# A decoder layer on one core: values spread by one copy each from ScalarE's queue, and two lags of the attention steps lengthened

## The chip, the cores and the metric

The kernel runs on one core of a Trainium2 chip. The metric is the device time of one execution in microseconds (us). TensorE (PE) multiplies, VectorE (DVE) and ScalarE (ACT) work on tiles of 128 partitions, GpSimd (POOL) does small vector work and issues accumulating transfers, and SyncE (SP) issues most transfers. ScalarE has a queue for transfers of its own.

## What is computed

One layer of a decoder trunk on 512 tokens of width 1024, all in float32. After a norm and one wide projection there are two mixers side by side, retention and a dilated attention in three groups of four heads; then an output projection, an MLP of width 4096 and a gated embedding term. The change touches the attention:

```python
for g, (window, dilation) in enumerate(((128, 1), (512, 4), (2048, 16))):
    # keys gathered by stride, own block and previous block, QK-norm and rotary before
    s = einsum(q_g, k_g) * hd ** -0.5          # masked to the window
    m = max(s); e = exp(s - m); l = sum(e)
    o_g = einsum(e / l, v_g); lse_g = m + log(l)
wts = softmax(stack(lse_g))                    # over the three groups
o = sum over g of wts_g * o_g                  # (512, 4 * 128)
```

All of it is in float32; where the kernel multiplies by weights, it does so in three products of operands split in a high and a low part.

## The kernel before, in words

**Products.** Each weight tile of 128x1024 floats (`raw`, 512 KB, loaded on SP at L212, for some with an addition by GpSimd's transfer at L228 or by DVE at L226) is split in two: ScalarE makes `whi` (L250), DVE then `wlo` = raw - whi (L251). Both have four buffers. A product is three matmuls (L262 to L264): whi, wlo, whi again with the other operand's low part. Many projections go by seven products of halves in place of eight (`seven_products`); a helper `after` takes each finished product out of its PSUM bank. Products have four PSUM banks (`pg`), and everything else (scores `sc`, transposes `pe`, `ph`, `pc`, weighted values `po`, and the products called `pa`) shares four others.

**Values.** `values_seven` makes the value rows for two groups at once. The part `m` of a product is finished by L757, L759 or L761, and for the products 6 and 7 the finished tile of 128 rows is spread by L764: every fourth row goes to another place in the 32 partitions of the strided value tile `v`, by four transfers of 32x512 floats (64 KB) each, on SP. It is called twice; each call has four such tiles, so that there are 32 transfers.

**Scores.** `scores(g, ...)` puts four blocks (`block(r)`) in a list of deferred steps. A block of groups 1 and 2 makes 128x512 scores in one bank (L787); group 0 has one such block and three of twice the width in two banks each (L795), seven banks in all. `softmax` masks them on DVE (L678, which frees the bank), takes the maximum (L681), scales it (L682, and L684 with the group before), and ScalarE makes exponentials `se` (L687, four of 128 columns or two of 256). `turn` transposes them (L694, four per block) when its lag is over; for group 2 it first forces `rescale`. `weigh_values` multiplies them with the values (L835).

**Rescaling.** `rescale(2, ...)` joins the groups' denominators: f (L863, its exponential on ScalarE at L864), w (L866), the sum (L867), the reciprocal `inv` (L870), f times inv (L871), and a copy `wide` (L878), all on DVE; ScalarE scales the last group's exponentials by inv, sixteen instructions at L876. TensorE transposes `wide` (`pc`, L884), ScalarE takes it out and writes it to DRAM (L886, L887), and reads it back spread over the partitions (L892); DVE multiplies the sum of the earlier groups by it (L897).

**What sets the order.** The program is written as one pass over the products. After each unit of product work `tick` advances a clock; deferred steps, put in by `later(lag, ...)` at the end of the list or by `prompt(lag, ...)` at its head, run when their lag is over, at most two for every two ticks. `force(key)` runs steps from the head of the list until the named one is done. A scheduler of the framework then arranges each engine's recorded instructions; that order is fixed when the kernel is built, and each engine runs its own list in order. ScalarE's rotation inputs `rz` (L987) and DVE's rotations (L575, L578, L580) are the retention keys' work, which lies beside.

Of the kernel before, what the change touches and what calls it, by code (L numbers as in the profile page):

```python
# [17 lines left out]
P = 128  # L18
S = 512
D = 1024  # L20
NT = S // P
# [6 lines left out]
DIL = 4  # L28
# [51 lines left out]
class Block:  # L80
# [618 lines left out]
    def attention(self):  # L699

        nc = self.nc
        with self.tc.manual_schedule(engines={nc.scalar.engine, nc.vector.engine}):
            qk = self.att_proj(0, 0), self.att_proj(0, 1)
        nc.sync.dma_start(self.mask, self.a["c_mask"])
        self.gain_rows(1, NG)
        self.rot_rows(1)
        self.spare = True
        self.left = self.token_factors_seven()
        rq = self.rq
        qk1 = self.att_proj(1, 0), self.att_proj(1, 1)  # L710
        pT = [self.big("pT") for _ in range(2)]
        first, turned = self.scores(0, *qk, rq, None, pT)
        strided = self.const.tile([P, NT, 2, H], F32, name="st0p")
        self.prompt(10, lambda: self.to_strided(first, strided))
        past, turned1 = self.scores(1, *qk1, self.rq, strided, None, 18)
        self.later(24, lambda: self.rescale(1, strided, past), ("past", 1))
        v0, v1 = self.values_seven((self.r, self.r_minus))
        for g, v, pTs, lag in ((0, v0, turned, 2), (1, v1, turned1, 8)):
            values = self.weigh_values(g, v, pTs)
            for r in range(NT):  # L720
                self.later(lag, lambda r=r, values=values: values(r), ("att", g, r))
        qk = self.att_proj(2, 0), self.att_proj(2, 1)
        last, turned = self.scores(2, *qk, self.rq, past, None, 14)
        self.later(21, lambda: self.rescale(2, past, last), ("past", 2))
        dec, kdec = self.decays()
        kd, v2 = self.values_seven((None, self.r_minus), self.ret_keys(kdec))
        values = self.weigh_values(2, v2, turned)
        for r in range(NT):
            self.later(5, lambda r=r, values=values: values(r), ("att", 2, r))
        return dec, kd  # L730

    def values_seven(self, scale, ready=None):

        nc = self.nc
        for j in range(2):
            self.force(("S", j))
        held, out = {}, {}

        def tile(n):
            if n not in out:  # L740
                out[n] = self.big("v")
            return out[n]

        def after(m, p, ps):
            t = p if m in (1, 2, 3, 6) else 2 + p
            main = m in (1, 2, 4)
            r = scale[0 if main else 1]
            by = {} if r is None else dict(scale=r[:, t : t + 1])
            if main:
                o = tile(0)[:, t]  # L750
            elif m in (3, 5):
                o = self.tmp("m3") if m == 3 else self.tabp.tile([P, 512], F32, tag="tab", name=self.nm("m5"))
                held[{3: 6, 5: 7}[m], p] = o
            else:
                o = held.pop((m, p))
            if m in (1, 3, 5, 4):
                nc.scalar.activation(o, ps, AF.Copy, **by)  # L757
            elif r is None:
                nc.vector.tensor_tensor(o, o, ps, op=ALU.add)  # L759
            else:  # L760
                nc.vector.scalar_tensor_tensor(o, ps, r[:, t : t + 1], o, op0=ALU.mult, op1=ALU.add)  # L761
            if m in (6, 7):
                for q in range(DIL):
                    nc.sync.dma_start(tile(1)[32 * t : 32 * (t + 1), q], o[q : P : DIL])  # L764
            if m in (2, 4) and ready is not None:
                ready(t, o)

        self.seven_products(self.left, after)
        return tile(0), tile(1)

    def scores(self, g, qT, kT, rq, past, held=None, lag=2):

        nc = self.nc
        st = self.const.tile([P, NT, 2, H], F32, name=f"st{g}")
        pTs = [[] for _ in range(NT)]
        self.es = {}
        slots = None if held is None else [b[:, i] for b in held for i in range(4)]

        def block(r):
            m, l = st[:, r, 0], st[:, r, 1]  # L780
            rs = slice(r * P, (r + 1) * P)
            es = []
            wide = g == 0 and r > 0
            if not wide:
                sc = self.bank("sc")
                for h in range(H):
                    nc.tensor.matmul(sc[:, h * P : (h + 1) * P], qT[:, h, rs], kT[:, h, rs], start=True, stop=True)  # L787
                es.append(self.softmax(sc, P, H, self.mask[:, 128 * (g + 1) : 128 * (g + 2)], rq[:, r], m, l,
                                       None if past is None else past[:, r, 0]))
                self.es[g, r] = es[0]  # L790
            else:
                for hp in range(2):
                    sc = self.bank("sc")
                    for h in range(2):
                        nc.tensor.matmul(sc[:, h * 256 : (h + 1) * 256], qT[:, 2 * hp + h, rs],  # L795
                                         kT[:, 2 * hp + h, (r - 1) * P : (r + 1) * P], start=True, stop=True)
                    hs = slice(2 * hp, 2 * hp + 2)
                    es.append(self.softmax(sc, 256, 2, self.mask[:, 0:256], rq[:, r, hs], m[:, hs], l[:, hs]))
            for e in es:
                self.later((5, 8, 11)[g], lambda e=e: turn(e, r), ("pT", g, r))  # L800

        def turn(e, r):
            if g == 2:
                self.force(("past", 2))
            if g == 1 and not self.pT1:
                self.pT1.append(self.big("pT"))
            out = slots.pop(0) if slots else self.pT1[0][:, r] if g == 1 else None
            pTs[r].append(self.transpose4(e, out))

        for r in range(NT):  # L810
            self.later(lag, lambda r=r: block(r), ("sc", g, r))
        return st, pTs
# [43 lines left out]
    def rescale(self, g, past, st):  # L856

        nc = self.nc
        for r in range(NT):
            self.force(("sc", g, r))  # L860
        t3 = lambda s: self.sm.tile([P, NT, H], F32, tag="sm16", name=self.nm(s))
        f, l = t3("f"), st[:, :, 1]
        nc.vector.tensor_tensor(f, st[:, :, 0], past[:, :, 0], op=ALU.subtract)  # L863
        nc.scalar.activation(f, f, AF.Exp)  # L864
        w = t3("w")
        nc.vector.tensor_tensor(w, f, past[:, :, 1], op=ALU.mult)  # L866
        nc.vector.tensor_tensor(l, l, w, op=ALU.add)  # L867
        if g == NG - 1:
            inv = t3("inv")
            nc.vector.reciprocal(inv, l)  # L870
            nc.vector.tensor_tensor(f, f, inv, op=ALU.mult)  # L871
            for r in range(NT):
                e = self.es[g, r]
                for h in range(H):
                    c = slice(h * P, (h + 1) * P)
                    nc.scalar.activation(e[:, c], e[:, c], AF.Copy, scale=inv[:, r, h : h + 1])  # L876
        wide = self.const.tile([P, H * NT], F32, name=f"wide{g}")
        nc.vector.tensor_copy(wide.rearrange("p (h r) -> p r h", h=H), f)  # L878
        d = self.dram.tile([H, S], F32, name=f"f_dram{g}", tag=f"f_dram{g}")
        spread = []  # L880

        def turn():
            ps = self.bank("pc")
            nc.tensor.transpose(ps[: H * NT, :P], wide, self.ident)  # L884
            turned = self.turned[: H * NT]
            nc.scalar.activation(turned, ps[: H * NT, :P], AF.Copy)  # L886
            nc.scalar.dma_start(d.rearrange("a (r l) -> (a r) l", r=DIL), turned)  # L887

        def load():
            spread.append(self.big("fb"))  # L890
            for h in range(H):
                nc.scalar.dma_start(spread[0][:, h], d[h : h + 1].to_broadcast([P, S]))  # L892

        def scale():
            for h in range(H):
                o = self.oT[0][:, h]
                nc.vector.tensor_tensor(o, o, spread[0][:, h], op=ALU.mult)  # L897

        self.later(1, turn)
        self.later(4, load)  # L900
        self.later(12, scale, ("scaled", g))


# [613 lines left out]
```

## Time and profile before

| | |
|---|---|
| median of 3 runs | 953.83 us (953.59 to 954.54) |
| profiled execution | 955.36 us |
| its span | 953.6 us |
| mean granted TensorE clock | 0.997 |

In the profile, L12 is line 12 of the kernel before. Busy shares are of the span; a row of the timeline has its start, its duration, the engine, the line, what it writes and from what, how many instructions it stands for, and in brackets how long the engine stood idle before it and what ended that. The part of the name behind the engine tells the queue: SPq and ACTq are transfers issued by SyncE and ScalarE, and their duration is that of issuing.

### The profile page before, as it was taken

How to read it: one execution, taken by the hardware profiler on the slowest of the kernel's cores; microseconds unless marked ns; L12 is line 12 of the kernel's file. 1: busy time of each engine (PE TensorE's matmuls, PEld its weight loads, DVE VectorE, ACT ScalarE, POOL GpSimd, SP SyncE). 2: the span in 40 equal slices, each digit the busy share in tenths (PEclk: the TensorE clock that was granted, in tenths of full speed). 3: DMA queues.
4: the chain of work that ended last, by engine and by line, in shares of the span. 5: the costliest groups of instructions: out<-in, count | busy, mean ns of one | idle time of the engine just before them, and what ended most of it. 6: DMA issues, size and time to landing. Idle time of an engine off the chain costs nothing.

```text
span 953.6 us, 14325 instructions
## 1 busy us (share of the span) xinstructions
PE 943.3 (99%) x5357; PEld 826.2 (87%) x5357; DVE 718.4 (75%) x997; ACT 562.1 (59%) x1065; POOL 159.5 (17%) x140
## 2 busy tenths in 40 slices
PE   9999999999899999999999999999999999999998
PEld 6888888888788888999988888988998998998887
DVE  7789964766697849386937889799499689769953
ACT  5657775445745566576714446884494486467651
POOL 0322210222001112223012211111212302112100
PEclk9999999999999999999999999999999999999999
DMA  9953466258437645869737677868958968876911
GB/s 333 282 170 82 106 141 215 64 118 195 148 111 155 173 100 138 163 181 217 232 115 236 148 178 214 206 153 222 199 156 202 191 183 157 224 172 159 288 50 56
DMA packets 92549, 162.87 MB, mean 171 GB/s; under 512 B 8608, under 2 KB 20544, under 8 KB 92480
## 3 DMA queue, kind: packets, MB, share of 16 engines
q1 hardware_dynamic: 65168, 113.37, 36.4%
q0 software_dynamic: 23936, 46.14, 29.0%
q10 hardware_dynamic: 3376, 2.44, 0.9%
q8 instruction: 42, 0.69, 0.3%
q14 instruction: 27, 0.22, 0.1%
HBM read 153.49 MB, written 6.34 MB: 168 GB/s over the span
## 4 chain that ended last, share of the span: by engine, by line
PE 92%; DVE 3%; ACT 1%; issue 1%; DMA 1%; POOL 1%; SPq 0%; ACTq 0%; POOLq 0%; DVEq 0%
PE pg L264 25%; PE pg L262 25%; PE pg L263 25%; PE pa L264 3%; PE pa L263 3%; PE pa L262 3%; PE po L835 1%; PE ph L590 1%; DVE wlo L251 1%; PE pe L694 1%; PE sc L787 1%; PE ry L1083 1%; PE kv L1070 1%; PE ry L1085 1%; DVE ro L578 0%
## 5 line engine op out<-in xcount | busy, mean ns | idle before, releaser
L251 DVE TENSOR_TENSOR wlo<-raw,whi 128x1024 fp32r<-128x1024 f32 (+1 forms) x258 | 306.8, 1198 | 112.7 <-ACT whi L250 111.8
L250 ACT ACTIVATE whi<-raw 128x1024 fp32r<-128x1024 f32 (+1 forms) x257 | 266.3, 1041 | 212.1 <-PE pg L264 87.2
L263 PE MATMUL pg<-f,whi 128*128 128x256 f32 x384 | 108.7, 283 | 0.0
L264 PE MATMUL pg<-f,wlo 128*128 128x256 f32 x384 | 108.7, 283 | 0.0
L262 PE MATMUL pg<-f,whi 128*128 128x256 f32 x384 | 108.7, 283 | 0.0
L262 PE MATMUL pg<-whi,hh 128*128 128x512 f32 x248 | 98.6, 398 | 0.0
L264 PE MATMUL pg<-whi,hl 128*128 128x512 f32 x248 | 97.1, 392 | 0.0
L263 PE MATMUL pg<-wlo,hh 128*128 128x512 f32 x248 | 96.8, 390 | 0.0
L262 PE MATMUL pg<-whi,f 128*128 128x512 f32 x192 | 75.4, 393 | 0.0
L263 PE MATMUL pg<-wlo,f 128*128 128x512 f32 x192 | 74.8, 389 | 0.0
L264 PE MATMUL pg<-whi,f 128*128 128x512 f32 x192 | 74.8, 389 | 0.0
L262 PEld LDWEIGHTS pg<-f,whi 128*128 128x128 f32 x384 | 73.7, 192 | 0.2
L263 PEld LDWEIGHTS pg<-f,whi 128*128 128x128 f32 x384 | 73.7, 192 | 0.2
L264 PEld LDWEIGHTS pg<-f,wlo 128*128 128x128 f32 x384 | 73.7, 192 | 0.0
L228 POOL DMA_DIRECT2D raw<-in_w_in x32 | 38.9, 1216 | 197.8 <-DVE wlo L251 193.0
L264 PEld LDWEIGHTS pg<-whi,hl 128*128 128x128 f32 x248 | 46.6, 188 | 9.8
L263 PEld LDWEIGHTS pg<-wlo,hh 128*128 128x128 f32 x248 | 46.6, 188 | 9.2
L262 PEld LDWEIGHTS pg<-whi,hh 128*128 128x128 f32 x248 | 46.6, 188 | 9.2
L228 POOL DMA_DIRECT2D raw<-in_w_down x24 | 29.0, 1215 | 139.3 <-DVE wlo L251 108.2
L262 PE MATMUL pg<-whi,us 128*128 128x512 f32 x128 | 52.1, 407 | 0.0
L228 POOL DMA_DIRECT2D raw<-in_w_up x24 | 29.0, 1211 | 135.0 <-DVE wlo L251 124.7
L264 PE MATMUL pg<-whi,us 128*128 128x512 f32 x128 | 50.0, 391 | 0.0
(280 smaller groups left out, 2298.0 us busy)
## 6 DMA issues: line engine op xcount, KB each, us to landing
raw<-in_w_in SPq DMA_DIRECT2D x72, 512.0 KB, 4.1
raw<-in_w_in POOLq DMA_DIRECT2D x32, 512.0 KB, 6.2
raw<-in_w_up SPq DMA_DIRECT2D x32, 512.0 KB, 4.6
raw<-in_w_down SPq DMA_DIRECT2D x32, 512.0 KB, 4.6
raw<-in_w_up POOLq DMA_DIRECT2D x24, 512.0 KB, 6.6
raw<-in_w_down POOLq DMA_DIRECT2D x24, 512.0 KB, 5.9
x<-in_x SPq DMA_DIRECT2D x8, 512.0 KB, 8.2
raw<-in_w_ret_out SPq DMA_DIRECT2D x8, 512.0 KB, 3.8
```

Source lines behind the costliest of these rows:

```text
L228: self.nc.gpsimd.dma_start(raw, self.chained[i].rearrange("(k p) n -> p k n", p=P), accum_op=ALU.add)
L250: self.pin(nc.scalar.activation(R(hi[:, i]), raw[:, i], AF.Copy))
L251: nc.vector.tensor_tensor(R(lo[:, i]), raw[:, i], hi[:, i], op=ALU.subtract)
L262: t.matmul(ps, sh, mh, start=first, stop=False, skip_group_check=more)
L263: t.matmul(ps, sh, ml, start=False, stop=False, skip_group_check=more)
L264: t.matmul(ps, sl, mh, start=False, stop=last, skip_group_check=more)
L590: self.nc.tensor.transpose(ps[:, t * P : (t + 1) * P], rots[t][:, h * HD : (h + 1) * HD], self.ident)
L694: self.nc.tensor.transpose(ps[:, k * P : (k + 1) * P], e[:, k * P : (k + 1) * P], self.ident)
L787: nc.tensor.matmul(sc[:, h * P : (h + 1) * P], qT[:, h, rs], kT[:, h, rs], start=True, stop=True)
L835: nc.tensor.matmul(po[:, h * P : (h + 1) * P], v[:, vt, h * HD : (h + 1) * HD], pt, start=b == 0, stop=b == len(blocks) - 1)
L1070: nc.tensor.matmul(ps, kd[:, n, hs], v[:, n, c], start=True, stop=True)
L1083: nc.tensor.matmul(y, sT[0][:, r], v[:, i, c], start=True, stop=i == 0)
```

## The change

There are four edits. Group 0's scores have a lag of 4 in place of 2. A finished value tile is spread by one transfer of 32x4x512 floats in place of four, as a prompt step with lag 2, from ScalarE's queue. The transposes of the last group's exponentials have a lag of 15 in place of 11. And `scale`, in `rescale`, first forces the weighing steps of the group before; as a new line it moves all later lines of the file by one (L898 was L897).

```diff
--- before.py
+++ after.py
@@ -709,7 +709,7 @@
         rq = self.rq
         qk1 = self.att_proj(1, 0), self.att_proj(1, 1)
         pT = [self.big("pT") for _ in range(2)]
-        first, turned = self.scores(0, *qk, rq, None, pT)
+        first, turned = self.scores(0, *qk, rq, None, pT, 4)
         strided = self.const.tile([P, NT, 2, H], F32, name="st0p")
         self.prompt(10, lambda: self.to_strided(first, strided))
         past, turned1 = self.scores(1, *qk1, self.rq, strided, None, 18)
@@ -760,8 +760,8 @@
             else:
                 nc.vector.scalar_tensor_tensor(o, ps, r[:, t : t + 1], o, op0=ALU.mult, op1=ALU.add)
             if m in (6, 7):
-                for q in range(DIL):
-                    nc.sync.dma_start(tile(1)[32 * t : 32 * (t + 1), q], o[q : P : DIL])
+                rows = tile(1)[32 * t : 32 * (t + 1)]
+                self.prompt(2, lambda: nc.scalar.dma_start(rows, o))
             if m in (2, 4) and ready is not None:
                 ready(t, o)
 
@@ -797,7 +797,7 @@
                     hs = slice(2 * hp, 2 * hp + 2)
                     es.append(self.softmax(sc, 256, 2, self.mask[:, 0:256], rq[:, r, hs], m[:, hs], l[:, hs]))
             for e in es:
-                self.later((5, 8, 11)[g], lambda e=e: turn(e, r), ("pT", g, r))
+                self.later((5, 8, 15)[g], lambda e=e: turn(e, r), ("pT", g, r))
 
         def turn(e, r):
             if g == 2:
@@ -892,6 +892,7 @@
                 nc.scalar.dma_start(spread[0][:, h], d[h : h + 1].to_broadcast([P, S]))
 
         def scale():
+            self.force(("att", g - 1, NT - 1))
             for h in range(H):
                 o = self.oT[0][:, h]
                 nc.vector.tensor_tensor(o, o, spread[0][:, h], op=ALU.mult)
```

Together with the scheduler this rearranges TensorE, DVE and ScalarE between some 101 and 330 us; SP only loses its 32 transfers, and GpSimd keeps its order. Numbers behind names only tell buffers apart, and differ between the two programs.

First ScalarE, at the last group's exponentials (`se` from L687), beside the splits of weights (`whi`). Before:

```order
L687 ACTIVATE se_2356,st_2159<-sm_2355,st_2159,rqs_1928 128x128 x4
L250 ACTIVATE whi_2459<-raw_2006 128x1024
L687 ACTIVATE se_2372,st_2159<-sm_2371,st_2159,rqs_1928 128x128 x4
L250 ACTIVATE whi_2463<-raw_2169 128x1024
L687 ACTIVATE se_2415,st_2159<-sm_2414,st_2159,rqs_1928 128x128 x4
L250 ACTIVATE whi_2557<-raw_2555 128x1024
L250 ACTIVATE whi_2563<-raw_2561 128x1024
L687 ACTIVATE se_2431,st_2159<-sm_2430,st_2159,rqs_1928 128x128 x4
L864 ACTIVATE f_2484<-f_2484 128x16
L987 ACTIVATE rz_2512<-v_2217,dec 128x128 x3
L876 ACTIVATE se_2356<-se_2356,inv_2490 128x128 x4
L876 ACTIVATE se_2372<-se_2372,inv_2490 128x128 x4
```

The two rows that follow there are the other scalings, then one more rz. After:

```order
L687 ACTIVATE se_2396,st_2147<-sm_2395,st_2147,rqs_1916 128x128 x4
L250 ACTIVATE whi_2441<-raw_1994 128x1024
L687 ACTIVATE se_2431,st_2147<-sm_2430,st_2147,rqs_1916 128x128 x4
L250 ACTIVATE whi_2445<-raw_2157 128x1024
L864 ACTIVATE f_2462<-f_2462 128x16
L988 ACTIVATE rz_2490<-v_2205,dec 128x128 x4
L764 DMA v_2381<-m_2227 32x4x512
L876 ACTIVATE se_2344<-se_2344,inv_2468 128x128 x4
L876 ACTIVATE se_2360<-se_2360,inv_2468 128x128 x4
L876 ACTIVATE se_2396<-se_2396,inv_2468 128x128 x4
L876 ACTIVATE se_2431<-se_2431,inv_2468 128x128 x4
L988 ACTIVATE rz_2515<-v_2205,dec 128x128 x4
```

The next rows there are whi_2528 and whi_2534. The splits whi_2441 and whi_2445 are what whi_2459 and whi_2463 were, and whi_2528 is what whi_2557 was: the first pair has moved behind the exponentials of block 2 and 3 (se_2396, se_2431) and the other split from ahead of block 3's exponentials to behind all sixteen scalings and two sets of rz. One spreading copy stands ahead of the scalings; two more stand some rows earlier, ahead of the exponentials of blocks 0 and 1, and the fourth is two rows behind whi_2534.

Next DVE, at the masking of blocks 2 and 3 (`sm`) and the start of rescale. Before:

```order
L678 TENSOR_TENSOR sm_2430<-sc_2425,mg_110 128x512
L761 SCALAR_TENSOR_TENSOR m_2239<-pg_2172,r_more,m_2239 128x512
L681 TENSOR_REDUCE mx_2433<-sm_2430 128x4
L251 TENSOR_TENSOR wlo_2558<-raw_2555,whi_2557 128x1024
L682 SCALAR_TENSOR_TENSOR st_2159<-mx_2433,rqs_1928 128x4
L761 SCALAR_TENSOR_TENSOR m_2247<-pg_2179,r_more,m_2247 128x512
L684 TENSOR_TENSOR st_2159<-st_2159,st_1123 128x4
L251 TENSOR_TENSOR wlo_2564<-raw_2561,whi_2563 128x1024
L863 TENSOR_TENSOR f_2484<-st_2159,st_1123 128x16
L226 TENSOR_TENSOR raw_2755<-raw_2755,raw_2749 128x1024
L866 TENSOR_TENSOR w_2487<-f_2484,st_1123 128x16
L867 TENSOR_TENSOR st_2159<-st_2159,w_2487 128x4x4
```

After:

```order
L761 SCALAR_TENSOR_TENSOR m_2227<-pg_2160,r_more,m_2227 128x512
L678 TENSOR_TENSOR sm_2395<-sc_2390,mg_110 128x512
L681 TENSOR_REDUCE mx_2398<-sm_2395 128x4
L682 SCALAR_TENSOR_TENSOR st_2147<-mx_2398,rqs_1916 128x4
L684 TENSOR_TENSOR st_2147<-st_2147,st_1123 128x4
L678 TENSOR_TENSOR sm_2430<-sc_2425,mg_110 128x512
L761 SCALAR_TENSOR_TENSOR m_2235<-pg_2167,r_more,m_2235 128x512
L681 TENSOR_REDUCE mx_2433<-sm_2430 128x4
L682 SCALAR_TENSOR_TENSOR st_2147<-mx_2433,rqs_1916 128x4
L684 TENSOR_TENSOR st_2147<-st_2147,st_1123 128x4
L863 TENSOR_TENSOR f_2462<-st_2147,st_1123 128x16
L251 TENSOR_TENSOR wlo_2442<-raw_1994,whi_2441 128x1024
```

Block 2's masking (sm_2395) now stands behind m_2227, which takes out the first of two banks of `us` products; before, it stood some rows ahead of both. wlo_2460 stood ahead of block 3's masking, and wlo_2442 stands behind all of it. Behind these rows after has wlo_2446, w, L575, L867, a half of L578, inv (L870), the other half, L871, L580, wide, and then the addition L226, which before stands ahead of w, inv and wide.

Last TensorE, at the transposes. Before:

```order
L263 MATMUL pg_2179<-wlo_2464,hh_146 128x512
L884 MATMUL pc_2551<-ident,wide_2509 16x128
L264 MATMUL pg_2179<-whi_2463,hl_148 128x512
L694 MATMUL pe_2598<-ident,se_2356 128x128 x2
L262 MATMUL pg_2616<-hh_145,whi_2557 128x512
L694 MATMUL pe_2598<-ident,se_2356 128x128 x2
L263 MATMUL pg_2616<-hl_147,whi_2557 128x512
L694 MATMUL pe_2605<-ident,se_2372 128x128
```

After:

```order
L263 MATMUL pg_2167<-wlo_2446,hh_146 128x512
L264 MATMUL pg_2167<-whi_2445,hl_148 128x512
L884 MATMUL pc_2552<-ident,wide_2487 16x128
L694 MATMUL pe_2633<-ident,se_2344 128x128 x4
L694 MATMUL pe_2640<-ident,se_2360 128x128 x4
L694 MATMUL pe_2659<-ident,se_2396 128x128 x4
L262 MATMUL pg_2578<-hh_145,whi_2528 128x512
```

Three sets of four transposes, which read scaled exponentials, now follow each other, and the products with the next weight (whi_2528) stand behind them; before, they alternated with the products with whi_2557. The 24 products `pg<-whi,us` and the 24 with hh and hl that follow are the same in both.

Near 101 us TensorE has, before, three score banks ahead of 12 products `pg<-whi,us`, then two banks, one product, a bank, eight products and the last bank. After, it has the 12 products first, three banks, 12 products with hh and hl, and then four banks in a row.

## What the prediction was

> **What bounds the kernel now.** I read the page first, then the busy times by stretch, then the timeline of each engine around the two places where the change acts. The page's first line says who sets the time:
>
> ```profile
> PE 943.3 (99%) x5357; PEld 826.2 (87%) x5357; DVE 718.4 (75%) x997; ACT 562.1 (59%) x1065; POOL 159.5 (17%) x140
> ```
>
> TensorE is busy for 943.3 of 953.6 us. Its work isn't changed, so the change can win or lose only in what TensorE waits. Two stretches hold most of that wait and both are touched (columns: stretch, its length, busy time and count of PE, PEld, DVE, ACT, POOL, granted clock, DMA share, GB/s):
>
> ```profile
> 100.00:120.00 20.00, 19.18 (x94) 16.00 (x93) 18.22 (x33) 13.56 (x37) 5.07 (x4) 1.00 0.48 106
> 240.00:260.00 20.00, 16.98 (x74) 13.60 (x73) 12.09 (x23) 15.12 (x47) 0.00 (x0) 0.91 0.47 152
> ```
> ```profile
> 250.00:255.00 5.00, 3.09 (x14) 2.24 (x12) 2.21 (x4) 2.77 (x12) 0.00 (x0) 1.00 0.31 91
> 255.00:260.00 5.00, 3.89 (x16) 3.09 (x17) 0.82 (x5) 4.37 (x15) 0.00 (x0) 0.66 0.60 210
> ```
>
> Near 108 us TensorE waits for score banks; near 253 us it stands for 3 us and then runs at a granted clock of 0.66. TensorE's timeline at the first place:
>
> ```profile
> 106.48 1.89 PE L795 MATMUL sc<-hT,hT 128*128 128x256 f32 x8
> ...
> 108.02 0.58 PE L262 MATMUL pg<-whi,hh 128*128 128x512 f32 x1
> ...
> 109.42 1.13 PE L795 MATMUL sc<-hT,hT 128*128 128x256 f32 x4 [0.82 <-DVE sm L678]
> ...
> 110.20 0.58 PE L263 MATMUL pg<-wlo,hh 128*128 128x512 f32 x1
> ```
>
> Behind the product at 108.02 the next start is due one product's step later, at 108.25 (the step follows below); the scores start at 109.42. TensorE loses 1.2 us to a score bank that the masking L678 of an earlier block still holds. At the second place:
>
> ```profile
> 242.28 0.39 PE L262 MATMUL pg<-whi,us 128*128 128x512 f32 x1
> ...
> 244.77 0.39 PE L264 MATMUL pg<-whi,us 128*128 128x512 f32 x1
> ...
> 247.72 0.39 PE L262 MATMUL pg<-whi,hh 128*128 128x512 f32 x1
> ...
> 252.70 0.39 PE L263 MATMUL pg<-wlo,hh 128*128 128x512 f32 x1
> ...
> 256.11 0.37 PE L884 MATMUL pc<-ident,wide 128*16 128x128 f32 x1 [3.02 <-DVE wide L878]
> ...
> 261.59 0.60 PE L694 MATMUL pe<-ident,se 128*128 128x128 f32 x4
> ```
>
> Products start every 0.227 us (242.28 to 247.72 are 24). The one at 252.70 should be followed at 252.93; the transpose pc comes at 256.11, 3.18 us late, for `wide`. Why `wide` is late stands on DVE:
>
> ```profile
> 246.10 0.74 DVE L761 SCALAR_TENSOR_TENSOR m<-pg,r_more,m 128x512 f32<-128x512 f32 x1
> ...
> 247.70 1.23 DVE L251 TENSOR_TENSOR wlo<-raw,whi 128x1024 fp32r<-128x1024 f32 x1 [0.27 <-ACT whi L250]
> ...
> 253.73 1.22 DVE L226 TENSOR_TENSOR raw<-raw,raw 128x1024 f32<-128x1024 f32 x1 [2.79 <-DMA v<-m]
> 254.88 0.17 DVE L866 TENSOR_TENSOR w<-f,st 128x16 f32<-128x16 f32 x1
> ...
> 255.28 0.25 DVE L870 RECIPROCAL inv<-st 128x16 f32<-128x16 f32 x1
> ...
> 255.78 0.18 DVE L878 COPY wide<-f 128x16 f32<-128x16 f32 x1
> 260.74 0.69 DVE L575 TENSOR_TENSOR ro<-rz,rotc 128x512 f32<-128x512 f32 x1 [4.78 <-ACT rz L987]
> 261.35 0.75 DVE L578 TENSOR_TENSOR ro<-rz,rotc 128x256 f32<-128x256 f32 x2
> ```
>
> The weight addition L226 waits 2.79 us for transfers, with w, inv and wide queued behind it.
>
> **What the change removes.** The wait at 108 goes, since the scores come later: -1.2. The stall at 253 goes too, whatever the copies do: in the new order `wide` stands ahead of L226. That is -3.18 idle and, with it, the low clock: (1 - 0.66) x 5.00 = 1.7, taken as -1.6. Together -6.0.
>
> The copies themselves: 32 issues on SP become 8 on ScalarE's queue.
>
> ```profile
> 246.87 7.26 SPq L764 DMA_DIRECT2D v<-m  x8
> ```
> ```profile
> DMA to landing us min/median/max: 2.0/4.2/7.1
> ```
> ```profile
> 260.90 0.33 ACTq L887 DMA_DIRECT2D f_dram<-turned  x1
> ```
>
> No row shows the 32x4x512 copy on ACT. Its issue is bounded by ACT's own small one, 0.3 us, and the four of a tile on SP, 7.26 / 2 = 3.6; I take 0.9 (7.26 / 8, one issue). In the new order two stand just ahead of exponentials that wait for DVE, one ahead of the scalings, which wait for inv, so that I count 0; without that cover each would cost its 0.9. The landing is read by the weighing products of the last group (count, durations in ns, first and last start):
>
> ```profile
> L835 PE MATMUL po<-pT,v x32: 270/275/275, 269.8 to 276.9; 128*128 128x128 f32 x32
> ```
>
> The last copy stands on ScalarE's queue two places behind whi_2528, for which the walk below has 263.7: with 1.06 and 0.6 for these, 0.9 for the issue and even 7.1 to land, 273.4, against 269.8 and the 5 us of stall that the walk adds: hidden, 0. If it landed 3 us later still, that would be what it costs. The forced step in scale() only fixes an order: 0.
>
> **What it adds near 101 to 123.** Twelve products now run before the scores; the seven score blocks then stand in two clusters, the last four in a row, on four banks. DVE's rows:
>
> ```profile
> 102.17 0.74 DVE L578 TENSOR_TENSOR ro<-pg,S 128x256 f32<-128x256 f32 x2
> ...
> 111.21 0.68 DVE L678 TENSOR_TENSOR sm<-sc,mg 128x512 f32<-128x512 f32 x1
> ...
> 111.92 0.69 DVE L681 TENSOR_REDUCE mx<-sm 128x2 f32<-128x512 f32 x1
> ...
> 112.65 0.16 DVE L682 SCALAR_TENSOR_TENSOR st<-mx,rq 128x2 f32<-128x2 f32 x1
> 112.72 0.68 DVE L678 TENSOR_TENSOR sm<-sc,mg 128x512 f32<-128x512 f32 x1
> ```
>
> The second product bank is free only when L578 ends, at 102.91; TensorE now wants it after six products, 101.12 + 6 x 0.227 = 102.48: +0.4. A block takes DVE 1.51 us (111.21 to 112.72) and TensorE 0.5; the cluster of four runs ahead, and the bank of an old block is waited for. Bounds: 0 (other products cover it) and two blocks, 3.0. I take 1.0, near the 1.2 that this same wait costs now. Together +1.4.
>
> **What it adds near 247 to 264.** This is the term that decides. ScalarE takes its instructions in order. In the new order the split whi_2441, which TensorE needs for the 24 hh products, stands behind the exponentials of block 2; their masking stands on DVE behind m_2227, which waits for the first 12 us products. Before, only the splits' own inputs and an earlier block stood ahead. ScalarE's rows give the prices:
>
> ```profile
> 246.60 1.06 ACT L250 ACTIVATE whi<-raw 128x1024 fp32r<-128x1024 f32 x1
> ...
> 249.76 0.50 ACT L687 ACTIVATE se<-sm,st,rqs 128x128 f32<-128x128 f32 x1 [0.73 <-DVE st L684]
> ...
> 251.69 0.20 ACT L864 ACTIVATE f<-f 128x16 f32<-128x16 f32 x1
> 251.80 0.97 ACT L987 ACTIVATE rz<-v,dec 128x128 f32<-128x128 f32 x3
> 255.63 4.79 ACT L876 ACTIVATE se<-se,inv 128x128 f32<-128x128 f32 x16 [2.86 <-DVE inv L870]
> 260.33 0.39 ACT L987 ACTIVATE rz<-v,dec 128x128 f32<-128x128 f32 x1
> ```
>
> Four exponentials: 251.69 - 249.76 = 1.93. Sixteen scalings: 260.33 - 255.63 = 4.70. Four rz: 4/3 x 0.97 = 1.29. Now the walk, on before's clock (the shift of everything earlier cancels):
> - The 12th us product starts at 244.77 and ends at 245.16. m_2227 0.66 (246.10 to L681's place), masking 0.71 (111.21 to 111.92), maximum 0.73, L682 and L684 0.2 each: exponentials from 247.7, to 249.6, whi_2441 to 250.7.
> - TensorE wants it at 247.72: **3.0 us of stall**. It does two products, then needs wlo_2442 (1.22 after whi): 251.94 against 251.17, **0.8**.
> - ScalarE: block 3's exponentials 1.93, whi_2445 1.06, f 0.2, rz 1.29: 255.2. DVE then puts L575 (0.61), L867 (0.2) and half of L578 (0.37) ahead of the reciprocal, and inv reaches ScalarE 0.35 later (255.28 to 255.63): 256.7.
> - Sixteen scalings 4.70, four rz 1.29, whi_2528 1.06: 263.7. TensorE has only pc and twelve transposes until it needs whi_2528.
>
> Without stalls TensorE would be there at 247.72 + 24 x 0.227 + 0.2 + 12 x 0.11 (four transposes in 0.60, the last one's own time off) = 254.7. So the chain costs 263.7 - 254.7 = 9.0 in all, the 3.0 and 0.8 in it. wlo_2529 stands behind L575 and L578 of the second rz: 262.7 + 0.61 + 0.75 + 1.22 = 265.2 against 264.6, +0.6. **Sum +9.6**; I take 9.4, since a row's steps overlap by some hundredths at ten joints.
>
> Does the clock fall again? After the first gap a slow stretch is hidden, as TensorE soon waits for scalings anyway. After the second it is not. The twelfth scaling ends at 256.7 + 11 x 0.294 + 0.39 = 260.3, the last transpose of its block 0.1 later, and whi_2528 at 263.7: a gap of 3.3 us. The row of before, with 3.18 us idle and 0.66 behind it, says that this is enough: 1.6. Nothing else in the trace shows how the fall depends on the gap, so the bounds are 0 and 1.6, and I take 0.8.
>
> The Trainium skill, "TensorE: Matmul & The Clock Gate", Part 1 (What's actually happening), has the array at half rate only after an idle window of about 3.4 us, windows that run freely, whatever the kernel does. By that rule a gap of 3.3 us need not fill a window, and the sum would go without this term, to 958.6; by the row it would be 960.2. The trace speaks against a strict reading, since 3.18 us were enough once.
>
> **The sum.** -6.0 + 1.4 + 9.4 + 0.8 = +5.6. On the profiled execution, 955.36 (span 953.6 and 1.8 around it), that is 961.0. The median of the three runs is 953.83, 1.5 below; on it the forecast is 959.4. The nearest to no change that a measurement of this kernel tells apart is 0.2%, 1.9 us.
>
> **The rivals.**
> - *Both old waits go and the new order is hidden* (faster). For it block 2's exponentials must start by 243.7, so that whi_2441 is ready at 247.7, and inv must come by 254.7 - 7.05 = 247.7. It would give 953.8 - 6.0 + 1.4 = 949.2. For it: ScalarE is busy for 59% of the span, and DVE for 75%. Against it: the walk has block 2's exponentials 4 us and inv 9 us later than that. 0.06.
> - *Only the second stall comes*, if block 2's masking isn't held behind m_2227. Then f is ready at 251.9 as now, inv at 254.6 and whi_2528 at 261.7: 7.0 + 0.6 in place of 9.4, which gives 957.6, or down to 954.5 without the new waits near 102 to 123 and with 1.6 of overlaps. For it: m_2227 needs only the first 12 of the 24 us products. Against it: the DVE order. 0.12, a half of which is called no change.
> - *The loads stay late.* L226 waited 2.79 us here; in the new order it stands ahead of L575 and wlo_2529. If it waits as long again, TensorE waits some 2 us more: 961.4 to 962.5. For it: two 512 KB loads are still on SP. Against it: SP has no copies before them any more. 0.12.
> - *The clock in the second gap* stays full, 958.6, or falls, 960.2: both lie within the forecast's own range.
>
> ```profile
> raw<-in_w_in SPq DMA_DIRECT2D x72, 512.0 KB, 4.1
> ```
>
> The usual load lands in 4.1 us, so it is likelier that L226 finds its tiles.
>
> **How the numbers follow.** The two stalls as walked have 0.70, 957.6 to 961.4; the late loads 0.12; the second stall alone 0.12; the gain 0.06. The range 955.6 to 962.3 leaves out the gain, a half of the second-stall case and the tail of the late loads, about 0.17. Faster by over 0.2% (below 951.9): 0.06; within: 0.06; slower (above 955.7): 0.88.
>
> **What would show it.** Right: in the new trace no wait of pc for wide above 0.5 us; hh products that wait some 3 us for ACT whi L250 near 246; pe transposes that wait for ACT se L876; a second wait of 3 us for whi after the scalings; in 240 to 265 TensorE idle for 8 to 9 us in place of 3. Near 102 a wait for DVE L578. Wrong: those hh products following on without a gap, or a gap that ends with a transfer.

## The result and the profile after

The changed kernel takes 963.4 us (median of 4 runs, 962.58 to 964.29) against 954.03 us for the kernel before beside it (4 runs, 953.59 to 954.54). The ratio is 1.0098, with a 95% interval of 1.0081 to 1.0116: slower by 9.4 us, in the direction that was forecast, and above its range. The profiled execution is one of 962.58 us, with a span of 960.7.

TensorE's work is the same, so the loss is waiting. First the page's line of the changed kernel, then the view that adds up TensorE's waits (engine, operation, line, what ended the wait; us in total, times, longest):

```profile
PE 945.0 (98%) x5357; PEld 825.7 (86%) x5357; DVE 719.0 (75%) x997; ACT 562.4 (59%) x1065; POOL 159.5 (17%) x140
```
```profile
PE pg L262 <- ACT whi L250: 5.7, 2, 2.9
PE pg L262 <- DVE ro L1007: 1.8, 1, 1.8
```

Neither old wait is in the list: pc no longer waits for `wide`, nor a score for a bank. Near 101 to 123 us there are two short waits in place of the forecast 0.4 and 1.0: 0.34 us at 102.76, which the view puts down to L650 and not to L578, and 0.29 us at 123.03. Two waits for a split weight have come, as walked, and one for L1007 that no term of the forecast names. TensorE's timeline has the places:

```profile
250.44 0.50 PE L262 MATMUL pg<-whi,hh 128*128 128x512 f32 x1 [2.83 <-ACT whi L250]
...
251.71 0.80 PE L263 MATMUL pg<-wlo,hh 128*128 128x512 f32 x1 [0.53 <-DVE wlo L251]
...
262.90 0.50 PE L262 MATMUL pg<-hh,whi 128*128 128x512 f32 x1 [2.91 <-ACT whi L250]
...
264.49 0.50 PE L264 MATMUL pg<-hh,wlo 128*128 128x512 f32 x1 [0.39 <-DVE wlo L251]
...
296.06 0.50 PE L262 MATMUL pg<-whi,us 128*128 128x512 f32 x1 [1.83 <-DVE ro L1007]
```

ScalarE's timeline shows why the first two come. The exponentials of block 2 start at 247.43, released by DVE, and the split stands behind them; the next weight's split stands behind sixteen scalings and four rz:

```profile
247.43 0.49 ACT L687 ACTIVATE se<-sm,st,rqs 128x128 f32<-128x128 f32 x1 [2.38 <-DVE st L684]
...
249.35 1.04 ACT L250 ACTIVATE whi<-raw 128x1024 fp32r<-128x1024 f32 x1
...
255.93 3.64 ACT L876 ACTIVATE se<-se,inv 128x128 f32<-128x128 f32 x12 [1.40 <-DVE inv L870]
259.31 0.55 ACTq L764 DMA_DIRECT2D v<-m  x1
259.46 1.28 ACT L876 ACTIVATE se<-se,inv 128x128 f32<-128x128 f32 x4
260.62 1.28 ACT L988 ACTIVATE rz<-v,dec 128x128 f32<-128x128 f32 x4
261.79 2.01 ACT L250 ACTIVATE whi<-raw 128x1024 fp32r<-128x1024 f32 x2
```

The walk had 247.7, 249.6, 256.7 and, for the end of whi_2528, 263.7; the trace, which is 0.3 us ahead by then, has 247.43, 249.35, 255.93, and TensorE has the split by 262.90. Two signs that the prediction named did not come. No transpose is listed as waiting for L876, and the four waits between 240 and 265 us make 6.7 us of idle time, not 8 to 9: behind the first gap TensorE ran slowly (a granted clock of 0.67, shown below), so that it came to the transposes late enough.

The third wait is made on DVE. A weight addition L226 waits 5.32 us for its load and holds up all behind it; from there DVE works without a listed pause until 296 us, some 24 us, and L1007, which must free a product bank for TensorE, is late:

```profile
258.96 1.23 DVE L226 TENSOR_TENSOR raw<-raw,raw 128x1024 f32<-128x1024 f32 x1 [2.03 <-DMA raw<-in_w_in]
...
271.49 1.22 DVE L226 TENSOR_TENSOR raw<-raw,raw 128x1024 f32<-128x1024 f32 x1 [5.32 <-DMA raw<-in_w_in]
...
294.62 1.39 DVE L1007 TENSOR_TENSOR ro<-pg,rotc 64x512 f32<-64x512 f32 x2
```

### The profile page after: what moved, and what is told of

Read it like the earlier page. It is cut to its first block, busy times and chain, and to the rows that moved or that the text cites. A ratio compares the mean times of both kernels' runs of the same rounds, so it can differ in the third digit from the quotient of the medians.

```text
span 960.7 us, 14275 instructions
## 1 busy us (share of the span) xinstructions
PE 945.0 (98%) x5357; PEld 825.7 (86%) x5357; DVE 719.0 (75%) x997; ACT 562.4 (59%) x1065; POOL 159.5 (17%) x140
## 4 chain that ended last, share of the span: by engine, by line
PE 84%; DVE 7%; ACT 4%; DMA 2%; issue 2%; POOL 0%; ACTq 0%; SPq 0%; DVEq 0%; POOLq 0%
PE pg L262 23%; PE pg L264 23%; PE pg L263 23%; PE pa L264 3%; PE pa L263 3%; PE pa L262 3%; DVE wlo L251 2%; DMA raw<-in_w_down 1%; PE ph L590 1%; ACT se L687 1%; PE po L835 1%; ACT whi L250 1%; PE sc L787 1%; PE ry L1084 1%; DVE ro L1007 1%
## 5 line engine op out<-in xcount | busy, mean ns | idle before, releaser
L226 DVE TENSOR_TENSOR raw<-raw,raw 128x1024 f32<-128x1024 f32 x32 | 39.1, 1222 | 22.5 <-DMA raw<-in_w_in 18.1
L262 PE MATMUL pg<-whi,us 128*128 128x512 f32 x128 | 52.3, 408 | 2.2 <-DVE ro L1007 1.8
```

Source lines behind the costliest of these rows:

```text
L226: self.nc.vector.tensor_tensor(total, total, part, op=ALU.add)
L262: t.matmul(ps, sh, mh, start=first, stop=False, skip_group_check=more)
```

## The experiments

Times are medians; the ratio is to the kernel before on the same chip, with its interval. In the first four runs that kernel had a median of 953.48 us over 25 runs, in the second four 953.29 over 19, in the last four 953.15 over 7.

**One edit or all of them.** First the copy edit alone, on the kernel before:

```diff
-                for q in range(DIL):
-                    nc.sync.dma_start(tile(1)[32 * t : 32 * (t + 1), q], o[q : P : DIL])
+                rows = tile(1)[32 * t : 32 * (t + 1)]
+                self.prompt(2, lambda: nc.scalar.dma_start(rows, o))
...
         def scale():
+            self.force(("att", g - 1, NT - 1))
```

> The kernel before with the copy edit alone: one transfer of 32x4x512 per value tile from ScalarE's queue as a prompt step, and the forced step that it needs to build; both lags as before. Theory (the copies' place in ScalarE's list rearranges ScalarE and DVE, and that is the whole loss): 962 to 965 us, with a wait of about 3 us for ACT whi L250 near 247 and another of about 3 near 260, and the 1.2 us wait for a score bank near 108 as before. Rival (the longer lag of the last group's transposes makes the chain late): under 956 us, neither wait there.

Measured: 962.83 us, ratio 1.0106 (1.0088 to 1.0123), with both waits:

```profile
253.24 1.22 PE L262 MATMUL pg<-whi,hh 128*128 128x512 f32 x2 [2.83 <-ACT whi L250]
...
265.68 0.50 PE L262 MATMUL pg<-hh,whi 128*128 128x512 f32 x1 [2.95 <-ACT whi L250]
```

The copy edit alone carries the whole loss. Then the rest alone, that is the changed kernel with the four transfers on SP:

```diff
-                rows = tile(1)[32 * t : 32 * (t + 1)]
-                self.prompt(2, lambda: nc.scalar.dma_start(rows, o))
+                for q in range(DIL):
+                    nc.sync.dma_start(tile(1)[32 * t : 32 * (t + 1), q], o[q : P : DIL])
```

> The changed kernel with the four transfers per tile back on SP: both lags longer, the forced step kept. Theory: 953 to 955 us; no wait for whi, the stall of pc near 253 as before, some 0.1 us less near 101 to 137. Rival (lags): 959 us or more, with the transposes or the scalings late.

Measured: 952.78 us, ratio 0.9998 (0.9982 to 1.0014): both lags together are worth nothing that can be measured. One part of the expectation failed. In this profile pc waits 0.4 us, though DVE's list has the addition ahead of `wide` as before. So that order doesn't make a stall of 3 us in every execution.

```profile
253.35 0.27 PE L884 MATMUL pc<-ident,wide 128*16 128x128 f32 x1 [0.38 <-DVE wide L878]
```

**Queue, size or place of the copy.** One transfer in place of four, on SP at the old place:

```diff
-                for q in range(DIL):
-                    nc.sync.dma_start(tile(1)[32 * t : 32 * (t + 1), q], o[q : P : DIL])
+                nc.sync.dma_start(tile(1)[32 * t : 32 * (t + 1)], o)
```

> The kernel before with one transfer of 32x4x512 in place of four, still on SP and at the same place; all else as before. Theory (the addition L226 waits for a load that shares SP's queue with 16 spreading transfers): the load lands about 4 us after its issue, the stall of pc near 253 is under 0.5 us and the time is 948 to 951 us. Rival (the load is late for another reason, and the copies don't matter): the stall of 3 us stays, 953 to 955 us.

Measured: 954.76 us, ratio 1.0022 (1.0008 to 1.0036). The theory fell: with fewer transfers the time is no shorter. The profile is of the slowest of the ten runs (959.34 us). In it the addition waits for its load again, and the landing of the copies took 6.3 us in the middle, against 4.2 before:

```profile
256.06 1.23 DVE L226 TENSOR_TENSOR raw<-raw,raw 128x1024 f32<-128x1024 f32 x1 [3.18 <-DMA raw<-in_w_in]
```
```profile
DMA to landing us min/median/max: 4.1/6.3/8.5
```

Next the changed kernel with one word changed:

```diff
-                self.prompt(2, lambda: nc.scalar.dma_start(rows, o))
+                self.prompt(2, lambda: nc.sync.dma_start(rows, o))
```

> The changed kernel with one word changed: the copy's queue is SP's in place of ScalarE's; prompt step, lags and forced step stay. Theory (the place on ScalarE, not the step's place among the deferred ones): no wait for whi near 247 and 260, 949 to 955 us, the lower end where the loads land in time. Rival (the prompt steps take the turns of other deferred steps and so delay them): 960 us or more, as the changed kernel.

Measured: 951.86 us, ratio 0.9985 (0.9976 to 0.9995), ten runs between 951.15 and 952.34. TensorE's list of waits has none between 240 and 300 us. The queue's name decides over some 11 us (9.4 slower and 1.6 faster, each beside the kernel before); the prompt step costs nothing. The addition still stands ahead of `wide`, and finds its load in time:

```profile
249.25 1.22 DVE L226 TENSOR_TENSOR raw<-raw,raw 128x1024 f32<-128x1024 f32 x1
```

**The transfers, or the order that comes with them.** Two kernels take these apart. The first has transfers on ScalarE's queue and the good order: the copy on SP, and beside it a transfer of the same tile to a scratch place.

```diff
-                self.prompt(2, lambda: nc.scalar.dma_start(rows, o))
+                scratch = self.dram.tile([P, 512], F32, name=self.nm("scr"), tag="scr")
+                self.prompt(2, lambda: (nc.sync.dma_start(rows, o), nc.scalar.dma_start(scratch, o)))
```

> The changed kernel with the spreading copies on SP, and beside each of them one more transfer of the same tile from ScalarE's queue to a scratch place that nothing reads. ScalarE's list has transfers at the same two places ahead of the exponentials of blocks 0 and 1, but keeps the splits whi of the hh products and of the next weight ahead of blocks 2 and 3. Theory (the order costs, not the transfers): 951 to 954 us, no wait for ACT whi. Rival (issuing four transfers holds ScalarE): 956 us or more.

Measured: 952.96 us, ratio 0.9994 (0.9981 to 1.0007). ScalarE issues its transfers among the splits, the splits are early, and no product waits for one (a wait of 0.80 us for L1008, the line that is L1007 in the changed kernel, is there at 286.45):

```profile
238.60 0.33 ACTq L765 DMA_DIRECT2D scr<-m  x1
...
242.81 1.05 ACT L250 ACTIVATE whi<-raw 128x1024 fp32r<-128x1024 f32 x1
...
246.56 0.34 ACTq L765 DMA_DIRECT2D scr<-m  x1
246.63 1.04 ACT L250 ACTIVATE whi<-raw 128x1024 fp32r<-128x1024 f32 x1
```

The second has the late splits, and no copy on ScalarE's queue:

```diff
-                self.prompt(2, lambda: nc.scalar.dma_start(rows, o))
+                self.prompt(2, lambda: nc.sync.dma_start(rows, o))
...
-        kd, v2 = self.values_seven((None, self.r_minus), self.ret_keys(kdec))
+        with self.tc.manual_schedule(engines={nc.scalar.engine}):
+            kd, v2 = self.values_seven((None, self.r_minus), self.ret_keys(kdec))
```

> The changed kernel with the copies on SP, and ScalarE alone in the order in which the program is written while the last values are made: no transfer stands on its queue there, but the splits for the hh products stand behind the exponentials of blocks 2 and 3, and the next weight's split behind all sixteen scalings and eight rz. Theory (the order costs): 957 to 962 us with a wait of about 3.5 us for ACT whi L250 after the scalings; the first wait is shorter than in the changed kernel, under 1.5 us, since the us products' splits are late too. Rival (without transfers on ScalarE's queue there is no loss): 951 to 954 us.

Measured: 962.95 us, ratio 1.0103 (1.0083 to 1.0123), just above the range given for it. TensorE's waits there:

```profile
248.89 0.50 PE L263 MATMUL pg<-wlo,hh 128*128 128x512 f32 x1 [0.57 <-DVE wlo L251]
...
259.31 0.80 PE L262 MATMUL pg<-hh,whi 128*128 128x512 f32 x1 [3.45 <-ACT whi L250]
...
294.20 0.50 PE L262 MATMUL pg<-whi,us 128*128 128x512 f32 x1 [1.51 <-DVE ro L1008]
```

So an order with late splits makes a loss of this size without the transfers, and the transfers without it make none. The order isn't quite that of the changed kernel, and the loss is made up otherwise: the first stall is 0.57 us in place of 2.83, the second is longer, and the granted clock is 0.50 for 6.8 us from 257.9 on.

**One stall without the other.** The copy's step at lag 4 (`prompt(4, ...)` in the changed kernel) brings the hh products' splits forward and leaves the next weight's behind the scalings.

> The changed kernel with the copy's step at lag 4 in place of 2, still on ScalarE's queue. In ScalarE's list the splits for the hh products then stand ahead of block 2's exponentials, and the next weight's split is still behind the scalings. Theory (two stalls, each from one place in the list): no wait for whi near 247; the pc transpose and the scalings come earlier, the wait for whi after the scalings is 2 to 3 us, a wait for DVE wlo of up to 3 us follows near 272; 957 to 962 us. Rival (one cause behind both): either both waits stay, 962 us or more, or both go, under 955 us.

Measured: 964.78 us, ratio 1.0118 (1.0093 to 1.0144). The waits are those expected: none for whi near 247, then

```profile
254.35 0.27 PE L884 MATMUL pc<-ident,wide 128*16 128x128 f32 x1 [1.12 <-DVE wide L878]
...
259.96 0.80 PE L262 MATMUL pg<-hh,whi 128*128 128x512 f32 x1 [1.93 <-ACT whi L250]
...
278.23 0.50 PE L264 MATMUL pg<-hh,wlo 128*128 128x512 f32 x1 [2.82 <-DVE wlo L251]
```

The two stalls are two places in the list. The time is 3 us above the range given. The clock fell for longer there, which is the likely reason (columns as in the prediction):

```profile
255.00:260.00 5.00, 3.07 (x11) 1.61 (x11) 1.01 (x3) 5.00 (x16) 0.00 (x0) 0.59 0.25 52
260.00:265.00 5.00, 5.00 (x12) 3.89 (x13) 5.00 (x9) 3.13 (x8) 0.00 (x0) 0.50 0.44 142
```

The first row is hidden, as TensorE waits for the split until 259.96. Behind the split the second row costs 0.50 x 5 = 2.5 us of full-speed time, and 280 to 285 us, with a clock of 0.68, another 0.32 x 5 = 1.6. In the changed kernel's profile no such row stands behind the second gap.

**A better version.** The copies on SP, and the scores at lag 5:

```diff
-        first, turned = self.scores(0, *qk, rq, None, pT, 4)
+        first, turned = self.scores(0, *qk, rq, None, pT, 5)
```

> The changed kernel with the copies on SP and group 0's scores at lag 5 in place of 4. Theory (from the walk over four banks: with one more product group between, the last score banks are free when wanted): 0.5 to 1.0 us less than the same kernel at lag 4, that is 950.5 to 951.5 us; TensorE's wait for DVE sm L678 near 122 under 0.25 us. Rival (the score banks are hidden either way): 951.5 to 952.5 us.

Measured: 952.01 us, ratio 0.9988 (0.9978 to 0.9998): as the rival has it, no different from lag 4. The wait near 122 did go, from 0.27 us at lag 4 to none that is listed, but it was too short to be seen in the time. Both versions on SP are faster than the kernel before by 0.12 to 0.15%, less than the 0.2% that was called measurable.

**Additions on GpSimd**, so that a late load holds up nothing on DVE, in three kernels (the changed one, the one before, and the one with copies on SP):

```diff
-                self.nc.vector.tensor_tensor(total, total, part, op=ALU.add)
+                self.nc.gpsimd.tensor_tensor(total, total, part, op=ALU.add)
```

> The changed kernel with the weight additions of L226 on GpSimd in place of DVE, so that an addition that waits for its load holds up nothing on DVE. The splits stand behind exponentials and scalings as in the changed kernel. Theory (the third wait, near 293 in the changed kernel, comes from DVE's backlog behind an addition that waited 5.3 us): no wait for DVE ro L1007 near 290, the two waits for ACT whi stay at about 3 us each; 960 to 962.5 us. Rival (the backlog has another source): that wait of 1 to 2 us stays, 963 us or more.

> The kernel before with the weight additions of L226 on GpSimd in place of DVE. Theory (the stall of pc near 253 is a late load under an addition that stands ahead of w, inv and wide on DVE, and most runs of the kernel before have little of it): no stall of pc over 0.3 us, the spread of the runs narrower, the slow ones of 956 us and more gone; median 951 to 953 us. Rival (DVE and GpSimd disturb each other, or the additions are late): 953.5 us or more.

> The changed kernel with the copies on SP and the weight additions of L226 on GpSimd. Theory (both sources of region-wide waits are gone; what is left is the first bank near 102): 950 to 951.5 us. Rival (nothing left to gain there): 951.5 to 952.5 us, as with the copies on SP alone.

Measured: 985.8 us, ratio 1.0338 (1.0319 to 1.0357); 977.05, 1.0257 (1.0215 to 1.0299); 978.99, 1.0268 (1.0232 to 1.0304). As a remedy this failed. An addition takes 2.6 us there, against 1.22 on DVE:

```profile
L226 POOL TENSOR_TENSOR raw<-raw,raw x32: 2349/2616/3386, 56.4 to 882.8; 128x1024 f32<-128x1024 f32 x32
```

The rival of the second expectation, that DVE and GpSimd disturb each other, shows in the traces. In the second of these kernels DVE's small L871, which takes 0.17 us in the kernel before, lasts until an addition on GpSimd ends:

```profile
256.96 2.35 POOL L226 TENSOR_TENSOR raw<-raw,raw 128x1024 f32<-128x1024 f32 x1 [23.41 <-DVE st L867]
```
```profile
257.16 2.19 DVE L871 TENSOR_TENSOR f<-f,inv 128x16 f32<-128x16 f32 x1
```

It isn't the only one. Without the 32 additions, 39 us at 1.22 each, DVE is busy for 732.1 us there against 718.4 before, so that its other instructions took some 53 us longer in all, by far most of it in instructions that overlap an addition. That GpSimd's list also holds the small powers that norms wait for, and the issues of accumulating loads, may add to the loss; how the loss divides wasn't tried. L871 stands ahead of `wide`, and pc waits 2.08 us in this kernel: the expectation of no stall there failed, and it leaves open what the stall would be without an addition on either engine.

For the third wait these kernels don't give a plain answer. In the first of the three, TensorE has the two waits for whi, 2.83 and 2.90 us long, and between the second and 320 us no other, where the changed kernel has 1.83 for DVE; so far this fits the theory. But the third of them, with early splits and no addition on DVE, has two waits for L1007, 1.12 us at 288.56 and 2.04 at 292.48. And in the experiment with the copy edit alone an addition waits 4.70 us at 273.64, and no such wait follows. An addition that waits is neither needed for the third wait nor enough for it.

**The kernel before, once more.**

> The kernel before, unchanged, for a second profile. Theory (its first profiled execution, 955.36 us, was one with an unusually long stall of pc near 253 and a clock of 0.66 behind it): pc waits under 1.5 us, the clock in 255 to 260 is 0.95 or more, 951.5 to 954.5 us. Rival (every execution has them): a stall of 3 us and 0.66 again.

Measured: 953.42 us, span 951.6. The stall is there at half its size, and the clock stays up:

```profile
254.54 0.27 PE L884 MATMUL pc<-ident,wide 128*16 128x128 f32 x1 [1.64 <-DVE wide L878]
```
```profile
250.00:255.00 5.00, 3.37 (x17) 2.48 (x16) 2.86 (x8) 3.52 (x16) 0.00 (x0) 1.00 0.42 99
255.00:260.00 5.00, 5.00 (x32) 4.12 (x31) 0.81 (x2) 5.00 (x18) 0.00 (x0) 1.00 0.51 190
```

A wait of 1.64 is a little over the bound given and far from the 3.02 of the first profile. Of the first 25 runs of this kernel beside the experiments, only the two slowest (956.97 and 957.37) had a mean clock of 0.998; all others had 0.999 or 1.0. The execution of the first profile had 0.997. So a fall of the clock behind this stall is rare; how long the stall is on average, two profiles don't tell.

## Why the prediction was right in kind and too low

**What held.** The direction; the mechanism; and the walk near 247 to 264. The second profile of the kernel before is the better measure for it. The same products start there and in the changed kernel at

```profile
247.53 0.39 PE L262 MATMUL pg<-whi,hh 128*128 128x512 f32 x1
```
```profile
276.72 0.39 PE L262 MATMUL pg<-hh,whi 128*128 128x512 f32 x1
```
```profile
325.97 0.38 PE L1070 MATMUL kv<-v,v 128*128 128x256 f32 x1
```

and, in the changed kernel, at 250.44 (above) and at

```profile
284.01 0.48 PE L262 MATMUL pg<-hh,whi 128*128 128x512 f32 x1
```
```profile
335.15 0.38 PE L1071 MATMUL kv<-v,v 128*128 128x256 f32 x1
```

so that the changed kernel is behind by 2.91, 7.29 and 9.18 us in this pair of executions. In the second figure the 1.64 us of pc's stall are gained back; the new waits are 7.29 + 1.64 = 8.9 us, against 9.4 forecast with a bounded 0.8 for the clock. Issuing transfers from ScalarE's queue costs nothing, as the fifth experiment shows (in the changed kernel a copy's issue takes 0.55 us, where 0.9 was bounded), no product in the changed kernel's list waits for a copy to land, and the lags cost nothing either: the -1.2 and +1.4 near 101 to 123 came out as nothing together (second experiment).

**What failed first: the size of what the change removes.** This is the term that was mis-sized. The prediction put the stall at 253 at -3.18 and the low clock behind it at -1.6. Both were read from one execution, and it was an unusual one. It noted that this execution was 1.5 us above the median, and then took the terms off the median whole. Its twin loses 1.64 us there and no clock. That is 3.1 us of gain that wasn't there to be had in it; without them the same sum would have come to 962.5 us.

**What failed second: the sum ended too early.** It stopped when TensorE had whi_2528 and wlo_2529. The delay goes on to the loads and back to DVE. In the changed kernel SP issues a load at 266.20, 0.03 us after DVE's wlo of 264.95 has ended, and the addition L226 starts at 271.49, when the load has landed; it has waited 5.32 us, and DVE, with no pause listed from there on, lets TensorE wait 1.83 us at 296, over 30 us behind the last step that was walked. That is the step from 7.29 to 9.18. The prediction had late loads as a rival, for another reason (a transfer still on its way at the first addition) and at another place, and gave it 2 us and a chance of 0.12. This chain is read from one execution and wasn't tried by itself: the experiments above show the third wait without a late addition, and a late addition without the third wait. What decides whether the wait comes stays open.

**The clock.** Forecast 0.8 between 0 and 1.6. In the changed kernel's profile it fell behind the first gap, where it is hidden, and not behind the second; in the first experiment, with the same two gaps, it did fall behind the second. The columns are those of the prediction, the first two rows are the changed kernel's, and the last is the first experiment's:

```profile
250.00:255.00 5.00, 4.03 (x10) 2.92 (x11) 2.94 (x4) 4.53 (x15) 0.00 (x0) 0.67 0.60 120
...
265.00:270.00 5.00, 5.00 (x23) 4.12 (x23) 1.17 (x2) 2.84 (x6) 0.00 (x0) 1.00 0.76 218
```
```profile
265.00:270.00 5.00, 3.94 (x11) 2.83 (x12) 3.95 (x6) 5.00 (x9) 0.00 (x0) 0.68 0.31 99
```

There the low clock costs TensorE some 1.6 us, and the third wait isn't there. A TensorE that comes later by that much finds most of a wait of 1.83 us gone, so the two terms need not add up; DVE's order differs a little there too, so this is argued and not shown. The changed kernel's profile is also of the fastest of its four runs: its mean clock is 0.997, and that of the other three 0.994 or 0.995. An estimate from these is (0.997 - 0.995) x 961 = 1.9 us of full-speed time that they lost and this profile did not; whether they had the third wait isn't recorded.

For the pair of profiles, together: +5.6 forecast, +3.1 for the gain that wasn't there, +1.9 for the third wait, -0.8 for the clock in this profile, -0.5 for the new waits and -0.2 near 101 give +9.1, where the traces have 9.18. The medians have 9.4; that the two agree so well is in part luck.

**The scheduler.** That the copy's queue moves the splits is shown, by the fourth experiment's one word. What in the framework's scheduler does it stays open: transfers to the scratch place from the same queue don't move them.

## What to carry to other kernels

A transfer put on a computing engine's queue may cost nothing to issue and still cost some 10 us, if the scheduler arranges that engine's work around it: compare the order of the engine's other instructions, and walk from what they now stand behind. A stall that a change is to remove should be taken from several executions, or at the size that fits the median, not from the one that was profiled. And a walk isn't over when the delayed engine has its operand: follow the buffer that it gives back late.

## What the runs showed of the hardware

A gap of some 3 us on TensorE may or may not lower the granted clock behind it: 2.91 us left it at 1.00 in one execution, 2.95 brought 0.68 in another. The record of the granted clock in these traces has it at 0.50 or 1.00 only, and each low stretch inside these two kernels' work lasts 3.41 us. What TensorE did in the 3.41 us just ahead of such a stretch was to be busy for 0.73 us (changed kernel, first gap) and 1.15 us (first experiment, second gap). The changed kernel's second gap lies across two such pieces of time, with 1.48 and 2.05 us of busy time in them, and the clock stayed. No bound can be drawn from this: in the experiment with the step at lag 4 a low stretch follows 3.41 us with 2.29 us of busy time, mostly transposes. The Trainium skill, "TensorE: Matmul & The Clock Gate", Part 1 (What's actually happening), has windows of about 3.4 us that run freely, whatever the kernel does, and half rate after an idle one. The traces agree with the length, 3.41 us, and with the free running, as the same gap falls both ways; that gaps of 2.9 us lower the clock shows that the window need not be idle throughout.

The start differs as well, where both programs are the same: in its first 10 us the changed kernel's profile has 26 matmuls, that of the first experiment 19, and the latter is some 2 us behind from there on:

```profile
0.00:10.00 10.00, 8.34 (x26) 4.89 (x27) 4.72 (x9) 5.39 (x9) 0.79 (x9) 1.00 0.80 252
```
```profile
0.00:10.00 10.00, 8.34 (x19) 4.57 (x20) 4.75 (x9) 5.44 (x9) 0.78 (x9) 1.00 0.80 252
```

While GpSimd adds two float32 tiles of 128x1024 (2.35 us), a DVE instruction beside it can last until the addition ends: one on 128x16 elements took 2.19 us in place of 0.17.
